# Two-layer decoder trunk on one core: three value products per key block in one bank, three score banks, no row sums on GpSimd

## The chip, the cores and the metric

The kernel runs on one core of a Trainium2 chip. The metric is device time in microseconds (us) of one execution, the median over several. Engines are called by the names of the profile: PE is TensorE (PEld its weight loads), DVE is VectorE, ACT is ScalarE, POOL is GpSimd, SP is SyncE, which issues most of the DMAs.

## What is computed

Two layers over 2048 tokens of width 1024. Layer 0 is a gated linear recurrence beside a pooling mixer. Layer 1 is causal attention with 16 heads of 64, where a key's weight also carries a forget term. The change touches layer 1 (and one helper that all weights pass). Cut to that:

```python
logf = jax.nn.log_sigmoid(fl + b_f)
cumf = jnp.cumsum(logf, axis=1).transpose(0, 2, 1)
...
logits = (jnp.einsum('bhqd,bhkd->bhqk', q[:, :, q0:q1], k[:, :, :q1]) * scale
          + cumf[:, :, q0:q1, None] - cumf[:, :, None, :q1])
mask = jnp.arange(q0, q1)[:, None] >= jnp.arange(q1)[None, :]
probs = jax.nn.softmax(jnp.where(mask, logits, -jnp.inf), axis=-1)
outs.append(jnp.einsum('bhqk,bhkd->bhqd', probs, v[:, :, :q1]))
...
o = o * jax.nn.silu(g)
return o @ w_out
```

## The kernel before, in words

The 2048 tokens go through in four segments of 512 (SEG). Each segment passes layer 0 and then layer 1, so the timeline alternates: a layer-0 stage of some 300 us, then an attention stage that grows with the segment, since segment s attends to s + 1 segments of keys.

Matrix products run in a format that keeps part of the mantissa (fp32r). To keep more of it, an operand is held as a first part (a rounded copy) and a second part (what the rounding left); a product of two such operands takes three matmuls. The helper `split_lo` (L184) makes a second part: full value minus first part. Its engine is DVE unless another is named.

**Weights.** `prep_w` brings one weight tile (1024 x 256) in four DMAs of 128 x 512 (`raw`). For each, ACT casts the first part (L295) and `split_lo` makes the second one. Pieces 1 and 3 of a tile go to POOL, pieces 0 and 2 to DVE (tile 0 wholly to POOL). Two tiles `wt` exist; `next_w` starts the load of the tile after the one that it hands out.

**Attention** (`attend`, L1116) runs per head over key blocks of 128 keys by 512 queries, 4(s + 1) blocks; the last four of a head lie on the diagonal and have 512, 384, 256 and 128 queries. Per block: two matmuls write the scores into a bank of PSUM (`pst`, two such banks; on the diagonal a third matmul adds the mask); ACT takes the exponential twice, once rounded (`ph`, L1153) and once in place (L1154); DVE subtracts to get the second part `pl`; two blocks later (LAG) the values are multiplied. The values are held with 130 columns: 64 second parts, 64 first parts and two columns of ones. Two products do it:

```python
mm(po[:, q0:], vv[:, b, 0:P], ph[:, q0:], start=(kb == 0), stop=end)
mm(pol[0:HD + 2, q0:], vv[:, b, HD:], pl[:, q0:],
   start=(kb == 0), stop=end)
```

The bank `po` (tile `pov`) then holds both halves of value x `ph` on separate partitions, and the bank `pol` first value x `pl` and, in a row of its own, the sum of `pl`. The sum of `ph` over the keys is kept apart: POOL adds each block's `ph` into `la` (L1160 to L1164), and the reduction over the 128 partitions is left to `finish`. At the end of a head DVE adds the row of `pol` to `la` (L1176) and puts the three value parts together (L1177, L1178), ACT rounds `la` (`lh`, L1180), and DVE makes its second part (`ll`). `finish` (L1184), run for a pair of heads, sums `lh` and `ll` of both heads over the partitions with four matmuls against `pairr` (`pL`), takes the reciprocal on ACT and multiplies.

**What goes on beside it.** `max_pass` does the scores of the next head with queries and keys changed about (`pmx`), from which DVE takes the row maximum (L1102, L1104). `prep` (L1054) makes the queries and keys of the head after that (ACT and DVE). `quad_attention` yields once per key block, and `weave` puts pieces of other projections between (`pqk`, `pgt`, `pv`, then `py`), in steps of 24 matmuls or 12. Within each engine the order is fixed when the program is built: a scheduler places instructions by priority and by its own estimate of when an operand is there.

**PSUM** has eight banks: two `pj` for projections, two `mx` (row maximum and small things), two `st`, one `o` and one `o2`. Layer 0 uses `st`, `mx` and `o` for the recurrence; `out_first` holds four banks for the first output tiles, one of them `o2`.

Of the kernel before, what the change touches and what calls it, by code (L numbers as in the profile page):

```python
# [35 lines left out]
def trunk(ctx, tc, x, cvec, norm_g, ada_c, ada_w, ada_b, ada_bg, lbp, w0, w0o, w1, w1f, w1o,  # L36
# [4 lines left out]
    def mm(*a, **k):  # L41
        return nc.tensor.matmul(*a, **k)  # L42
# [25 lines left out]
    def tmp(name, dt=F32, shape=(P, 512)):  # L68
        return tp.tile(list(shape), dt, name=name, tag="tmp")
# [5 lines left out]
        return ps.tile([P, 512], F32, name=name, tag="pj", bufs=2)  # L75

    def ps_st(name):
        return ps.tile([P, 512], F32, name=name, tag="st", bufs=2)

    def ps_o(name):  # L80
        return ps.tile([P, 512], F32, name=name, tag="o", bufs=1)

    def ps_o2(name):
        return ps.tile([P, 512], F32, name=name, tag="o2", bufs=1)

    def ps_mx(name):
        return ps.tile([P, 512], F32, name=name, tag="mx", bufs=2)
# [1 line left out]
    def f(ap):  # L89
        return ap.bitcast(F32)  # L90
# [21 lines left out]
    eps1 = cp.tile([P, 1], F32, name="eps1")  # L112
    V.memset(eps1, EPS)

    pairr = cp.tile([P, 3 * HD], F32R, name="pairr")
    of = tmp("of")[:, 0:3 * HD]
    V.memset(of, 0.0)
    V.memset(of[:, HD:2 * HD], 1.0)
    V.tensor_copy(pairr, of)

    NL = 7
    lmask = cp.tile([P, NL, P // 2], U8, name="lmask")
# [60 lines left out]
    def split_lo(out_t, full, hi, eng=None):  # L183
        (eng or V).tensor_tensor(out_t, full, f(hi), op=ALU.subtract)  # L184
# [93 lines left out]
    def prep_w(n):  # L278
        if n >= len(wseq) or n in wready:
            return  # L280
        late = wseq[n][0] == "e"
        src = None if late else wsrc[wseq[n][0]][wseq[n][1]]
        wt = wp.tile([P, 2, ND, 256], F32R, name="wt", tag="wt")
        parts = range(3 if late else 4)
        if not late and n >= len(wseq) - 5:
            parts = range((NEARLY[wseq[n][1]] + 1) // 2)
        for h in parts:
            sl = slice(2 * h, 2 * h + 2)
            raw = wp.tile([P, 2, 256], F32, name="raw", tag="raw", bufs=4)
            nc.sync.dma_start(raw, w1o[h][:, ND - 2:, :] if late else src[:, sl, :])  # L290
            if late:
                V.tensor_tensor(raw, raw, grow1[0][:, h * 256:(h + 1) * 256].unsqueeze(1).to_broadcast([P, 2, 256]),
                                op=ALU.mult)
            tc.cur_priority += 80
            S.copy(wt[:, 0, sl, :], raw)  # L295
            split_lo(wt[:, 1, sl, :], raw, wt[:, 0, sl, :], G if (h % 2 or n == 0) and n < len(wseq) - 2 else V)
            tc.cur_priority -= 80
        wready[n] = wt

# [520 lines left out]
    def out_first(s):  # L820

        L = seg0[s]
        xs = L["x"] = []
        for tb in range(NTB):
            xt = xp.tile([P, D], F32, name="xo", tag="xs")
            nc.sync.dma_start(xt, x[s * SEG + tb * P:s * SEG + (tb + 1) * P, :])
            xs.append((xt, once([P, 4], f"ss{tb}")))
        wt = next_w(("b", 0))

        L["py"] = wt, [(ps_pj, ps_pj, ps_o2, ps_mx)[tb]("py")[:, 0:256] for tb in range(NTB)]  # L830
        for tb in range(NTB):
            assert L["cores"] >= 3
            proj_N(L["py"][1][tb], wt, L["mix"], tb, (4, 5, 6, 7, 0, 1, 2), last=False)
            yield
# [281 lines left out]
    def attend(s, h):  # L1116
# [3 lines left out]
        Q1, Q3, K1, K2 = L["ops", h]  # L1120
        pair, j = h // 2, h % 2
        vc = L["v", pair]
        la = kp.tile([P, SEG], F32, name="la", tag="la", bufs=1)
        po, pol = ps_o("pov"), ps_o2("pol")
        nkb = NTB * (s + 1)
        kb = 0
        todo = []

        def values(b, q0, kb, vv, ph, pl):
            end = kb == nkb - 1  # L1130
            mm(po[:, q0:], vv[:, b, 0:P], ph[:, q0:], start=(kb == 0), stop=end)
            mm(pol[0:HD + 2, q0:], vv[:, b, HD:], pl[:, q0:],
               start=(kb == 0), stop=end)

        for c in range(s + 1):
            if c < s:
# [7 lines left out]
            for b in range(NTB):  # L1144
# [9 lines left out]
                S.activation(st[:, q0:], st[:, q0:], AF.Exp)  # L1154
                pl = tmp("pl", F32R)
                split_lo(pl[:, q0:], st[:, q0:], ph[:, q0:])
                if kb == 0:
                    first = f(ph)
                    if s == 0:
                        G.tensor_copy(la, first)  # L1160
                elif kb == 1 and s > 0:
                    G.tensor_tensor(la, first, f(ph), op=ALU.add)
                else:
                    G.tensor_tensor(la[:, q0:], la[:, q0:], f(ph[:, q0:]), op=ALU.add)  # L1164
                todo.append((b, q0, kb, vv, ph, pl))
                if len(todo) > LAG:
                    values(*todo.pop(0))
# [3 lines left out]
            values(*t)  # L1171
        if j == 0:
            L["u", pair] = xp.tile([P, 2, SEG], F32, name="u", tag="xs")
        u = L["u", pair][j * HD:(j + 1) * HD, 0, :]
        S.copy(u, po[HD:P])
        V.tensor_tensor(la[0:1], pol[HD:HD + 1], la[0:1], op=ALU.add)  # L1176
        V.tensor_tensor(u, po[0:HD], u, op=ALU.add)  # L1177
        V.tensor_tensor(u, pol[0:HD], u, op=ALU.add)  # L1178
        lh, ll = tmp("lh", F32R), tmp("ll", F32R)
        S.copy(lh, la)  # L1180
        split_lo(ll, la, lh)
        L["l", h] = (lh, ll)

    def finish(s, h):  # L1184

# [3 lines left out]
            return  # L1189
        u, rl = L["u", pair][:, 0, :], L["u", pair][:, 1, :]  # L1190
        pL = ps_misc("pL")
        for i in range(2):
            for part in range(2):
                mm(pL, pairr[:, (1 - i) * HD:(1 - i) * HD + P], L["l", h - 1 + i][part], start=(i + part == 0), stop=(i + part == 2))
        S.activation(rl, pL, AF.Ln)
        S.activation(rl, rl, AF.Exp, scale=-1.0)
        mix = L["mix"]
# [190 lines left out]
```

## Time and profile before

| | |
|---|---|
| median of 3 runs (lowest to highest) | 3030.41 us (3029.74 to 3030.75) |
| the profiled execution: its own time, its span | 3029.48 us, 3027.8 us |
| mean granted TensorE clock | 0.975 |
| busy: PE, PEld | 93%, 79% of the span |
| busy: DVE, ACT, POOL | 76%, 60%, 39% of the span |
| attention stages (us from the start) | 390 to 697, 998 to 1394, 1692 to 2172, 2473 to 3007 |

PE's matmuls are pipelined: a matmul of 512 columns is listed with some 0.4 us, but the next starts earlier; what one costs is read from start to start in the timeline. So a busy PE has losses in it that the idle time doesn't show. A weight load (PEld) goes with each matmul and carries the wait where the stationary operand is late. The granted clock has two levels in these records, 1.00 (2.4 GHz) and 0.50 (1.2 GHz); a mean between them is a mix of the two.

### The profile page before, as it was taken

Reading aid. Unit: us, or ns where it says so; the run is one execution under the profiler, and the core shown is the slowest. Engines: PE = TensorE matmul, PEld = TensorE weight load, DVE = VectorE, ACT = ScalarE, POOL = GpSimd, SP = SyncE. Lnnn points to the kernel's source line nnn. Section 1 sums busy time; section 2 is a strip of 40 time slices with the busy share of each in tenths; the row PEclk is TensorE's granted clock in tenths of the full one; section 3 lists DMA queues with packets and bytes.
Section 4 is the critical chain, followed back from the end, with each engine's and each line's share of the span. In section 5 each row is a group of like instructions: output and inputs, shape, how many; then the busy total and the mean of one; then the engine's idle time right before and its main releaser. Section 6 shows DMA issues by size and latency. Waiting matters only on the chain.

```text
span 3027.8 us, 49244 instructions
## 1 busy us (share of the span) xinstructions
PE 2808.9 (93%) x17212; PEld 2390.2 (79%) x17212; DVE 2301.3 (76%) x4390; ACT 1826.4 (60%) x3743; POOL 1172.5 (39%) x992
## 2 busy tenths in 40 slices
PE   4699999989999999989999999998999999999998
PEld 3688887879888887868878887776898877777777
DVE  8667678776676788886586788889667678888886
ACT  3344566774445666775455676768635467777774
POOL 3111233323211444444212355554432136566665
PEclk9899999999999999999999999999999999999999
DMA  7523365534233444533333443553342334333442
GB/s 246 174 57 102 106 141 139 119 91 124 79 102 110 119 119 104 131 99 115 100 95 116 122 124 115 126 133 113 97 126 71 114 104 115 105 113 107 113 138 86
DMA packets 207888, 348.97 MB, mean 115 GB/s; under 512 B 24068, under 2 KB 70788, under 8 KB 205080
## 3 DMA queue, kind: packets, MB, share of 16 engines
q1 hardware_dynamic: 201816, 329.03, 39.0%
q10 hardware_dynamic: 5824, 16.79, 1.7%
q8 instruction: 137, 2.24, 0.3%
q14 instruction: 111, 0.91, 0.1%
HBM read 293.58 MB, written 52.14 MB: 114 GB/s over the span
## 4 chain that ended last, share of the span: by engine, by line
PE 60%; DVE 19%; ACT 11%; DMA 4%; issue 4%; POOL 1%; SPq 0%; ACTq 0%; DVEq 0%; POOLq 0%
PE py L42 10%; PE pgt L42 8%; PE pqk L42 8%; PE pst L42 6%; PE pv L42 6%; PE pmx L42 4%; PE pov L42 3%; PE pol L42 3%; PE pf L42 3%; PE pq L42 3%; PE pl L42 3%; DVE pl L184 2%; DVE wt L184 2%; ACT wt L295 1%; DMA raw<-in_w_dram 1%
## 5 line engine op out<-in xcount | busy, mean ns | idle before, releaser
L184 POOL TENSOR_TENSOR wt<-raw,wt 128x512 fp32r<-128x512 f32 x287 | 419.5, 1470 | 1030.9 <-ACT wt L295 975.1
L1164 POOL TENSOR_TENSOR la<-la,ph 128x512 f32<-128x512 f32 (+3 forms) x528 | 610.6, 1156 | 385.7 <-ACT ph L1153 342.9
L184 DVE TENSOR_TENSOR pl<-pst,ph 128x512 fp32r<-128x512 f32 (+3 forms) x640 | 386.9, 605 | 133.4 <-ACT pst L1154 102.2
L1153 ACT ACTIVATE ph<-pst 128x512 fp32r<-128x512 f32 (+3 forms) x640 | 340.6, 532 | 235.1 <-PE pst L42 224.9
L42 PE MATMUL pqk<-wt,h 128*128 128x256 f32 x3072 | 433.1, 286 | 5.5 <-DVE h L497 2.7
L42 PEld LDWEIGHTS pqk<-wt,h 128*128 128x128 f32 x3072 | 411.9, 192 | 25.2 <-DVE h L497 3.5
L42 PE MATMUL pgt<-h,wt 128*128 128x512 f32 x1536 | 403.9, 405 | 0.0
L295 ACT CAST wt<-raw 128x512 fp32r<-128x512 f32 x578 | 335.2, 621 | 74.9 <-PE py L42 33.3
L42 PE MATMUL pv<-wt,h 128*128 128x256 f32 x2304 | 345.0, 298 | 10.7 <-DVE h L184 6.6
L42 PEld LDWEIGHTS pv<-wt,h 128*128 128x128 f32 x2304 | 326.1, 204 | 28.9 <-DVE h L184 9.6
L42 PEld LDWEIGHTS pgt<-h,wt 128*128 128x128 f32 x1536 | 293.1, 194 | 63.2 <-issue 1.9
L1154 ACT ACTIVATE pst<-pst 128x512 f32<-128x512 f32 (+3 forms) x640 | 340.0, 531 | 0.0
L184 DVE TENSOR_TENSOR wt<-raw,wt 128x512 fp32r<-128x512 f32 x291 | 265.7, 918 | 73.4 <-ACT wt L295 71.9
L1102 DVE TENSOR_REDUCE mxs<-pmx 128x1 f32<-128x512 f32 x384 | 258.6, 684 | 20.3 <-PE pmx L42 17.2
L42 PE MATMUL py<-wt,o 128*128 128x256 f32 x1536 | 202.2, 286 | 1.4 <-ACT o L1200 1.2
L42 PE MATMUL py<-wt,mix 128*128 128x256 f32 x1536 | 198.2, 287 | 2.3 <-DVE yt L844 2.1
L42 PEld LDWEIGHTS py<-wt,o 128*128 128x128 f32 x1536 | 192.8, 192 | 6.7 <-ACT o L1200 1.5
L42 PEld LDWEIGHTS py<-wt,mix 128*128 128x128 f32 x1536 | 187.9, 191 | 9.8 <-issue 4.5
L42 PE MATMUL pst<-Q,K1o 128*128 128x512 f32 x384 | 162.6, 424 | 23.2 <-DVE pl L184 21.7
L42 PE MATMUL pmx<-K2o,Q 67*128 67x512 f32 x384 | 162.0, 426 | 21.9 <-ACT Q L1077 10.2
L42 PE MATMUL pov<-ph,Vo 128*128 128x512 f32 x384 | 162.8, 425 | 6.6 <-ACT ph L1153 6.2
L1104 DVE CUSTOM_DVE_ANT_0 pmx<-pmx,mq 128x128 f32<-128x128 f32 (+3 forms) x256 | 124.6, 497 | 55.6 <-PE pmx L42 53.8
(251 smaller groups left out, 5309.1 us busy)
## 6 DMA issues: line engine op xcount, KB each, us to landing
raw<-in_w_dram SPq DMA_DIRECT2D x448, 256.0 KB, 3.5
K2o<-k2d SPq DMA_DIRECT2D x192, 160.0 KB, 3.4
Vo<-vd SPq DMA_DIRECT2D x96, 260.0 KB, 2.7
K1o<-k1d SPq DMA_DIRECT2D x96, 256.0 KB, 3.4
raw<-in_w1o_dram SPq DMA_DIRECT2D x66, 256.0 KB, 3.6
raw<-in_w0o_dram SPq DMA_DIRECT2D x64, 256.0 KB, 3.2
vd<-Vc SPq DMA_DIRECT2D x48, 260.0 KB, 8.1
ada<-in_ada_w_dram ACTq DMA_DIRECT2D x12, 1024.0 KB, 5.0
```

Source lines behind the costliest of these rows:

```text
L42: return nc.tensor.matmul(*a, **k)
L184: (eng or V).tensor_tensor(out_t, full, f(hi), op=ALU.subtract)
L295: S.copy(wt[:, 0, sl, :], raw)
L1102: V.tensor_reduce(mxs[:, i, c:c + 1], pm[:, 0:n], axis=AX.X, op=ALU.max)
L1104: V.tensor_tensor_reduce(pm[:, 0:n], pm[:, 0:n], mq[:, SEG - n:], 1.0, NEG, op0=ALU.add, op1=ALU.max, accum_out=mxs[:, i, c:c + 1])
L1153: S.activation(ph[:, q0:], st[:, q0:], AF.Exp)
L1154: S.activation(st[:, q0:], st[:, q0:], AF.Exp)
L1164: G.tensor_tensor(la[:, q0:], la[:, q0:], f(ph[:, q0:]), op=ALU.add)
```

## The change

Each key block has three value products, all into one bank: first parts of the values with the ones by `ph`, second parts by `ph`, first parts with the ones by `pl`. The bank then holds the finished values and the finished denominator in row 64, so POOL's adds, `la`, `pol` and the sums behind them go. At the end of a head ACT copies the denominator's first part and the values, and DVE makes the denominator's second part; both are rows of one tile `sums` (rows 0 and 32 for the even head, 64 and 96 for the odd one, zeros between), and `finish` needs one matmul. The bank that `pol` had becomes a third score bank; `out_first` takes a score bank in its place. From the fifth weight tile on, all second parts are made on POOL (the last two tiles of the list excepted).

```diff
     def ps_st(name):
-        return ps.tile([P, 512], F32, name=name, tag="st", bufs=2)
+        return ps.tile([P, 512], F32, name=name, tag="st", bufs=3)
...
-    def ps_o2(name):
-        return ps.tile([P, 512], F32, name=name, tag="o2", bufs=1)
...
-    pairr = cp.tile([P, 3 * HD], F32R, name="pairr")
-    of = tmp("of")[:, 0:3 * HD]
+    pairr = cp.tile([P, P], F32R, name="pairr")
+    of = tmp("of")
     V.memset(of, 0.0)
-    V.memset(of[:, HD:2 * HD], 1.0)
-    V.tensor_copy(pairr, of)
+
+    sums = cp.tile([P, SEG], F32R, name="sums")
+    V.tensor_copy(sums, of)
+    V.memset(of[0:HD, 0:HD], 1.0)
+    V.memset(of[HD:P, HD:P], 1.0)
+    V.tensor_copy(pairr, of[:, 0:P])
...
-            split_lo(wt[:, 1, sl, :], raw, wt[:, 0, sl, :], G if (h % 2 or n == 0) and n < len(wseq) - 2 else V)
+            split_lo(wt[:, 1, sl, :], raw, wt[:, 0, sl, :], G if (h % 2 or n == 0 or n >= NPRO) and n < len(wseq) - 2 else V)
...
-        L["py"] = wt, [(ps_pj, ps_pj, ps_o2, ps_mx)[tb]("py")[:, 0:256] for tb in range(NTB)]
+        L["py"] = wt, [(ps_pj, ps_pj, ps_st, ps_mx)[tb]("py")[:, 0:256] for tb in range(NTB)]
...
-        la = kp.tile([P, SEG], F32, name="la", tag="la", bufs=1)
-        po, pol = ps_o("pov"), ps_o2("pol")
+        po = ps_o("pov")
...
-            mm(po[:, q0:], vv[:, b, 0:P], ph[:, q0:], start=(kb == 0), stop=end)
-            mm(pol[0:HD + 2, q0:], vv[:, b, HD:], pl[:, q0:],
-               start=(kb == 0), stop=end)
+            mm(po[0:HD + 2, q0:], vv[:, b, HD:], ph[:, q0:], start=(kb == 0), stop=False)
+            mm(po[0:HD, q0:], vv[:, b, 0:HD], ph[:, q0:], start=False, stop=False)
+            mm(po[0:HD + 2, q0:], vv[:, b, HD:], pl[:, q0:], start=False, stop=end)
...
-                if kb == 0:
-                    first = f(ph)
-                    if s == 0:
-                        G.tensor_copy(la, first)
-                elif kb == 1 and s > 0:
-                    G.tensor_tensor(la, first, f(ph), op=ALU.add)
-                else:
-                    G.tensor_tensor(la[:, q0:], la[:, q0:], f(ph[:, q0:]), op=ALU.add)
...
-        u = L["u", pair][j * HD:(j + 1) * HD, 0, :]
-        S.copy(u, po[HD:P])
-        V.tensor_tensor(la[0:1], pol[HD:HD + 1], la[0:1], op=ALU.add)
-        V.tensor_tensor(u, po[0:HD], u, op=ALU.add)
-        V.tensor_tensor(u, pol[0:HD], u, op=ALU.add)
-        lh, ll = tmp("lh", F32R), tmp("ll", F32R)
-        S.copy(lh, la)
-        split_lo(ll, la, lh)
-        L["l", h] = (lh, ll)
+        r = j * HD
+        hi = sums[r:r + 1]
+        S.copy(hi, po[HD:HD + 1])
+        S.copy(L["u", pair][r:r + HD, 0, :], po[0:HD])
+        split_lo(sums[r + 32:r + 33], po[HD:HD + 1], hi)
...
-        for i in range(2):
-            for part in range(2):
-                mm(pL, pairr[:, (1 - i) * HD:(1 - i) * HD + P], L["l", h - 1 + i][part], start=(i + part == 0), stop=(i + part == 2))
+        mm(pL, pairr[0:97], sums[0:97], start=True, stop=True)
```

The scheduler gives PE another order. In the last attention stage, within one head, PE's rows were these (`pst` scores, `pov` and `pol` values, `pmx` the next head's row maximum, `pqk` a projection put between; an x stands before the number of equal rows):

```order
L42 MATMUL pst<-Q_28174,K1o 128x512
L42 MATMUL pst<-Q_28175,K2o 128x512
L42 MATMUL pol<-pl,Vo 66x512
L42 MATMUL pmx<-K2o,Q_28569 128x512
L42 MATMUL pov<-ph,Vo 128x512
L42 MATMUL pqk<-wt,h_25908 128x256
L42 MATMUL pst<-Q_28174,K1o 128x512
```

At the same place, PE's rows are now:

```order
L42 MATMUL pst<-Q_27775,K2o 128x512
L42 MATMUL pqk<-wt,h_25535 128x256 x24
L42 MATMUL pst<-Q_27774,K1o 128x512
L42 MATMUL pst<-Q_27775,K2o 128x512
L42 MATMUL pov<-ph,Vo 66x512
L42 MATMUL pov<-ph,Vo 64x512
L42 MATMUL pov<-pl,Vo 66x512
L42 MATMUL pmx<-K2o,Q_28160 128x512
L42 MATMUL pst<-Q_27774,K1o 128x512
```

A block has six matmuls of its own instead of five, and the projection's matmuls, which stood one to five at a time between the blocks, now stand in whole steps of 24 with several blocks between two steps.

POOL's rows at the beginning of the first attention stage were these:

```order
L184 TENSOR_TENSOR wt<-raw,wt 128x512 x12
L1160 COPY la<-ph 128x512
L184 TENSOR_TENSOR wt<-raw,wt 128x512 x2
L1164 TENSOR_TENSOR la<-la,ph 128x384
L1164 TENSOR_TENSOR la<-la,ph 128x256
L1164 TENSOR_TENSOR la<-la,ph 128x128
```

They are now (`Vc` is the ones beside the values of a pair of heads):

```order
L185 TENSOR_TENSOR wt<-raw,wt 128x512 x32
L1034 CAST Vc<-one_107 128x8x2
L185 TENSOR_TENSOR wt<-raw,wt 128x512 x8
L1034 CAST Vc<-one_107 128x8x2
L185 TENSOR_TENSOR wt<-raw,wt 128x512 x6
```

The row sums are gone from POOL's queue, and every piece of a weight tile is in it.

## Rows read from the trace of the kernel before

**Rows 1.** The page: busy time of each engine (1), the chain by engine (4).

```profile
PE 2808.9 (93%) x17212; PEld 2390.2 (79%) x17212; DVE 2301.3 (76%) x4390; ACT 1826.4 (60%) x3743; POOL 1172.5 (39%) x992
...
PE 60%; DVE 19%; ACT 11%; DMA 4%; issue 4%; POOL 1%; SPq 0%; ACTq 0%; DVEq 0%; POOLq 0%
```

**Rows 2.** Windows by stage: PE, PEld, DVE, ACT, POOL busy; clock, DMA share, GB/s.

```profile
390.00:697.00 307.00, 284.51 (x1836) 245.74 (x1834) 235.77 (x472) 213.27 (x448) 99.74 (x101) 0.98 0.46 117
697.00:998.00 301.00, 291.96 (x1991) 264.89 (x1990) 204.13 (x400) 141.06 (x294) 72.35 (x53) 0.98 0.38 108
998.00:1394.00 396.00, 366.30 (x2135) 302.41 (x2135) 314.20 (x588) 279.60 (x578) 174.18 (x150) 0.97 0.43 111
1692.00:2172.00 480.00, 448.00 (x2460) 358.72 (x2459) 396.84 (x715) 348.65 (x707) 257.46 (x214) 0.97 0.45 121
2473.00:3007.00 534.00, 509.26 (x2800) 402.81 (x2798) 451.35 (x805) 391.94 (x777) 341.63 (x277) 1.00 0.39 111
```

**Rows 3.** Timeline of PE, last attention stage: start, duration, what.

```profile
2605.25 0.28 PE L42 MATMUL pov<-ph,Vc 128*128 128x256 f32 x1
2605.37 0.27 PE L45 MATMUL pmt<-ident,m 128*1 128x128 f32 x1
...
2620.86 0.39 PE L42 MATMUL pst<-Q,K2o 67*128 67x512 f32 x1
2621.09 0.39 PE L42 MATMUL pol<-pl,Vo 128*66 128x512 f32 x1
2621.32 0.39 PE L42 MATMUL pov<-ph,Vo 128*128 128x512 f32 x1
```

**Rows 4.** Waits of PE's weight loads: us in total, times, longest.

```profile
PEld pst L42 <- DVE pl L184: 59.4, 78, 2.6
PEld pov L42 <- ACT ph L1153: 26.3, 73, 2.5
...
PEld pmx L42 <- ACT Q L1077: 20.4, 36, 1.7
PEld pol L42 <- DVE pl L184: 17.6, 41, 1.2
PEld pst L42 <- ACT Q L1114: 15.1, 32, 2.3
```

**Rows 5.** Windows in and after one stall in the second attention stage; columns as in rows 2.

```profile
1150.90:1153.30 2.40, 0.02 (x1) 0.00 (x0) 2.40 (x4) 1.76 (x4) 2.23 (x3) 1.00 0.68 184
1155.00:1157.00 2.00, 2.00 (x11) 2.00 (x11) 2.00 (x4) 0.32 (x1) 1.43 (x1) 0.50 0.54 135
```

**Rows 6.** Timeline of all engines across that stall.

```profile
1149.66 2.97 POOL L184 TENSOR_TENSOR wt<-raw,wt 128x512 fp32r<-128x512 f32 x2
...
1150.26 1.25 DVE L1199 TENSOR_TENSOR u<-u,sg 128x512 f32<-128x512 f32 x1
...
1151.43 1.24 DVE L172 TENSOR_TENSOR t_qk<-t_qk,ms_qk 128x16 f32<-128x16 f32 x1
...
1152.59 0.68 DVE L184 TENSOR_TENSOR pl<-pst,ph 128x512 fp32r<-128x512 f32 x1
...
1153.32 0.74 PE L42 MATMUL pst<-Q,K 128*128 128x512 f32 x2 [2.40 <-DVE pl L184]
```

**Rows 7.** Timeline of DVE in the third attention stage, while POOL does nothing.

```profile
1823.05 0.16 DVE L174 TENSOR_TENSOR ssq<-t_qk,r_qk 128x16 f32<-128x16 f32 x1
```

**Rows 8.** The page's groups (5): busy, mean ns of one, idle before.

```profile
L184 POOL TENSOR_TENSOR wt<-raw,wt 128x512 fp32r<-128x512 f32 x287 | 419.5, 1470 | 1030.9 <-ACT wt L295 975.1
L1164 POOL TENSOR_TENSOR la<-la,ph 128x512 f32<-128x512 f32 (+3 forms) x528 | 610.6, 1156 | 385.7 <-ACT ph L1153 342.9
...
L1153 ACT ACTIVATE ph<-pst 128x512 fp32r<-128x512 f32 (+3 forms) x640 | 340.6, 532 | 235.1 <-PE pst L42 224.9
...
L184 DVE TENSOR_TENSOR wt<-raw,wt 128x512 fp32r<-128x512 f32 x291 | 265.7, 918 | 73.4 <-ACT wt L295 71.9
```

**Rows 9.** Groups of DVE in the layer-0 stage from 697 to 998 us.

```profile
L184 DVE TENSOR_TENSOR wt<-raw,wt 128x512 fp32r<-128x512 f32 x39 | 34.5, 886 | 11.9 <-ACT wt L295 11.9
```

## The prediction

> **What bounds the kernel now.** The page first: PE is busy 93% of the span, DVE 76%, and 60% of the chain that ended last is PE, 19% DVE [rows 1]. So PE's work sets the time, and DVE is the engine that holds PE up. Next the windows by stage [rows 2]: in the four attention stages together (1717 us) PE is idle for 109 us (307 - 284.5, 396 - 366.3, 480 - 448.0, 534 - 509.3), while DVE is busy for 77 to 85% of each. In a layer-0 stage PE is idle for 9 of 301 us. Idle time is too little a measure, since a listed matmul hides the tail of the one before. The loads' waits show more [rows 4]: they waited 59.4 + 17.6 = 77.0 us for DVE's `pl`, 26.3 us for ACT's `ph` and 20.4 + 15.1 = 35.5 us for ACT's `Q`. Last the clock: the three earlier attention stages have a mean granted clock of 0.98, 0.97 and 0.97, the last one 1.00 [rows 2]. One stall shows how these hang together. PE waited 2.40 us for `pl` [rows 6], and DVE was busy all the while; a moment later, with PE at work again, the granted clock was 0.50, the 1.2 GHz level [rows 5]. DVE was late because of two jobs with both inputs in SBUF: a 128x16 product took 1.24 us and a 128x512 one 1.25 us beside a 2.97 us stretch of POOL [rows 6], while a 128x16 product took 0.16 us when POOL did nothing [rows 7].
>
> **What it costs PE.** From start to start, a matmul of 512 columns takes 0.23 us, with 66 stationary columns as with 128 [rows 3]; one of 256 takes 0.12 us [rows 3]. So a third product costs a whole matmul, though it has half the output. There are 640 key blocks: 16 heads x (4 + 8 + 12 + 16). Off the diagonal 384 x 0.23 = 88.3 us. On it, 64 of each width: 0.23 + 0.18 (between the two measured widths) + 0.12 + 0.12 (the 128 columns taken like 256) = 0.65, x 64 = 41.6 us; with 0.12 to 0.23 for the second and 0.06 to 0.12 for the last it is 34 to 45 us. `finish` loses three of four matmuls per pair: 32 x 3 x 0.23 = 22.1 us. Net **+108 us** (100 to 111). Nothing hides it, since PE is the path.
>
> **What it gives back in the attention stages.** The ceiling is what PE waits there.
> - `pl`, 77.0 us. With two banks the scores of block i + 2 wait for `pl` of block i; between stand one block's matmuls and the fills. With three, `pl` of block i is first needed by the third product, after the scores of i + 2: by the order that is 14 matmuls, 3.2 us, against two exponentials and a subtraction, 0.53 + 0.53 + 0.68 = 1.7 us [rows 6, 8] and three handovers. Before, eight matmuls and some fills (1.9 to 2.4 us) had to cover the same. DVE gets lighter too: 610.6 of POOL's 1172.5 us are row sums [rows 1, 8], and DVE's long products are long beside POOL's; at a head's end four DVE jobs become one. I take 65 us; bounds 0 and 77.
> - the clock: at 1.2 GHz half the time is lost, so a mean clock c loses (1 - c) of the stretch: 307 x 0.02 + 396 x 0.03 + 480 x 0.03 = 32.4 us. The dips follow the stalls, and the last stage has none. I take 24; bounds 0 and 32.
> - `Q`, 35.5 us: ACT's rounding of `la` no longer waits for POOL's last sum ahead of the next head's work. Part of the wait is ACT's own work. I take 18; bounds 0 and 35.5.
> - `ph`, 26.3 us: a third bank lets scores be made earlier, and there is a matmul more to cover the exponential. I take 16; bounds 0 and 26.3.
>
> Together 123 us (ceiling 171).
>
> **The other stages.** A layer-0 stage loses 39 splits on DVE, 34.5 us of its 204 [rows 2, 9]; POOL, busy for 72 of 301 us, gets 39 x 1.47 = 57 us more [rows 2, 8]. A weight tile then takes POOL 4 x 1.47 = 5.9 us, not 2.9, against 96 x 0.12 = 11.5 us of PE per tile, with the next tile loaded ahead: hidden, except where two tiles are taken at once (the last two of layer 0's output). PE's slack here is 9 us of idle and 6 us of clock (301 x 0.02); I take 1.5 us off each of three stages and nothing off the first (bounds: 15 us off each, 23 us on each). The ones for `v` (POOL's `Vc`) can hold weights behind them while a buffer is in use; that cover is the same 11.5 us per tile. The copies of single rows at a head's end take the place of whole-tile copies on ACT: nothing.
>
> **Sum.** Own time of the profiled execution 3029.5 (span 3027.8 and 1.7 around it; 0.9 under the median shown) + 108 - 123 - 4.5 = 3010 us.
>
> **Two rules of the skill.** Rows 6 and 7 show DVE's product stretched to the length of POOL's instruction. The Trainium skill, SBUF — State Buffer, "Who interferes with whom", states it as a lock: a DVE instruction with two SBUF inputs contends with a GpSimd instruction that reads SBUF, and the second to issue fully blocks until the first finishes. The trace agrees (1.24 us against 0.16 us). For attention this speaks for the change. For layer 0 it speaks against it, since 39 more POOL instructions per stage each may block a DVE product; that is rival 2. The stall and the clock [rows 5] agree with the Trainium skill, TensorE: Matmul & The Clock Gate, "What's actually happening": an idle PE is throttled to 1.2 GHz. By that rule alone all 32 us come back if the stalls go; I keep 24, since PE may still stall for other reasons, and the sum by the rule would be 3002 us.
>
> **The rivals.**
> 1. *PE's new order brings the waits back.* PE's row of six matmuls per block is 6 x 0.23 = 1.4 us. DVE needs `pl`, 0.68 us, and a row maximum of about the same length per block, 1.36 us. The projection's matmuls, which stood between the blocks, now come 24 at a time. In between, DVE has 0.04 us per block for keys, norms and gates; what it doesn't get done waits for the burst, and PE waits with it. Against it: about 1 us more of cover for `pl`. If only half of the 123 us comes back, the time is 3029.5 + 108 - 62 = 3075 us, slower. It decides if PE's loads still wait over some 40 us for `pl`.
> 2. *The lock moves to layer 0.* If each of 39 splits per stage blocks a DVE product for its 1.47 us, DVE does 57 - 34.5 = 23 us more per stage where the recurrence's products feed PE. With half of that on the path in four stages: 3010 + 46 = 3056 us, slower. For it: rows 6. Against it: DVE is busy for 68% there and PE's waits are short.
> 3. *All of it comes back.* With DVE under 75% and POOL nearly empty in attention, waits for `pl`, `ph` and the clock go wholly and those for `Q` mostly (160 us), and layer 0 gains 5 us a stage: 3029.5 + 108 - 160 - 15 = 2962 us. For it: the last stage runs at full clock already.
> 4. *Weights come late* where two tiles are taken at once: POOL's 5.9 us instead of 2.9 us in four stages, 3 us each: 3010 + 12 = 3022 us. This is also where the change does little.
>
> **How the numbers follow.** Forecast 52%, rivals 17, 9, 16 and 6%. A measurement of this kernel can tell about 0.2%, 6 us, from no change. Of the forecast's share some three quarters lie under 3024, the rest is split evenly; rival 3 is faster, 1 and 2 slower, 4 half faster and half within. Faster 0.57, within 0.12, slower 0.31. The range leaves out the end of rival 3 and the far half of rival 1: 2960 to 3072 us.
>
> **What would show it.** Right: waits of PE's loads for `pl` under 20 us, granted clock of at least 0.99 in all attention stages, no stretch in which a 128x16 product of DVE takes over 1 us there, PE's idle time in attention under 60 us although 544 matmuls more run. Attention stages: the first two shorter by some 10 us each, the third shorter by a few, the last longer by 10 to 20, since it has 256 of the 640 blocks and no lost clock to give back. Wrong: `pl` still over 40 us (rival 1), layer-0 stages over 310 us (rival 2), PE waiting for `wt` from POOL (rival 4), or matmuls of 66 or 64 stationary columns into the shared bank that take over 0.25 us from start to start, which would make the first term too small.

## The result: slower by 3.1%, and the profile after

| | before | after |
|---|---|---|
| median (lowest to highest) | 3030.58 us (3029.74 to 3039.66, 4 runs) | 3127.12 us (3122.61 to 3130.07, 4 runs) |
| ratio, 95% interval | | 1.0310 (1.0285 to 1.0335) |
| profiled execution: own time, span | 3029.48, 3027.8 us | 3122.61, 3120.8 us |

The forecast was 3010 us with a range up to 3072; the time lies 117 us over the one and 55 us outside the other. The page of after, beside [rows 1] and [rows 8]: busy time of each engine, the chain by engine and by line, the costliest group.

```profile
PE 2877.7 (92%) x17756; PEld 2426.0 (78%) x17756; DVE 1966.2 (63%) x3922; ACT 1823.0 (58%) x3743; POOL 819.5 (26%) x678
...
PE 52%; ACT 9%; issue 7%; DVE 7%; DMA 6%; POOL 2%; ACTq 0%; SPq 0%; POOLq 0%; DVEq 0%
PE pov L42 9%; PE pgt L42 7%; PE pqk L42 6%; PE pst L42 6%; PE py L42 6%; DMA K2o<-k2d 4%; PE pv L42 4%; PE pmx L42 4%; PE pf L42 2%; PE pq L42 2%; POOL wt L185 2%; PE pl L42 2%; DMA xt<-in_x_dram 1%; ACT wt L296 1%; ACT Q L1074 1%
...
L185 POOL TENSOR_TENSOR wt<-raw,wt 128x512 fp32r<-128x512 f32 x565 | 750.6, 1349 | 2061.6 <-ACT wt L296 1907.2
```

DVE lost 335 us and POOL 353 us of work, and the kernel is slower all the same. PE got 69 us more of listed work, and its share of the chain fell from 60 to 52%, so it isn't PE's added work alone. New among the costliest of the chain is a load, `K2o` (4%): the second of the two tiles in which a chunk of 512 stored keys is read back. It holds the keys' first parts and the rows of the forget term, and `pst` and the next head's `pmx` work with it.

Windows by stage (columns as in [rows 2]); the lines are attention and layer 0 in turn, the first layer-0 part (0 to 396) left out:

```profile
396.00:713.00 317.00, 290.52 (x1882) 251.23 (x1881) 176.48 (x394) 213.00 (x449) 86.80 (x71) 0.97 0.45 114
713.00:1025.00 312.00, 292.03 (x1991) 264.67 (x1991) 192.90 (x358) 141.37 (x293) 118.95 (x91) 0.98 0.36 105
1025.00:1415.00 390.00, 373.50 (x2245) 303.35 (x2244) 237.30 (x509) 279.10 (x579) 87.71 (x73) 0.99 0.42 113
1415.00:1725.00 310.00, 290.07 (x1973) 263.22 (x1972) 193.74 (x358) 139.47 (x290) 115.17 (x88) 0.97 0.36 104
1725.00:2215.00 490.00, 465.32 (x2628) 364.97 (x2627) 313.94 (x636) 346.96 (x706) 87.93 (x73) 0.99 0.43 118
2215.00:2526.00 311.00, 292.49 (x1983) 265.10 (x1982) 195.65 (x363) 140.38 (x291) 115.15 (x88) 0.97 0.33 99
2526.00:3098.00 572.00, 541.70 (x3009) 419.90 (x3008) 381.11 (x730) 390.40 (x777) 81.92 (x68) 0.99 0.36 104
```

Two things are to be seen. Every layer-0 stage is some 10 us longer though DVE has less to do there (193 us; 204 in [rows 2]). And the last attention stage took 572 us instead of 533, with 30 us in which PE is idle (25 before).

The waits of PE and its loads, beside [rows 4]:

```profile
PEld pst L42 <- DMA K2o<-k2d: 48.3, 37, 3.3
PE pst L42 <- DMA K2o<-k2d: 34.9, 33, 3.1
PE pl L42 <- DVE Dt L595: 32.8, 11, 4.8
PEld pov L42 <- DVE pl L185: 27.3, 62, 3.8
PEld pst L42 <- ACT Q L1115: 20.5, 35, 2.5
PEld pov L42 <- ACT ph L1153: 20.0, 24, 4.4
PEld pmx L42 <- ACT Q L1078: 14.6, 39, 1.0
```

The 77.0 us for DVE's `pl` are 27.3 now. Those for `Q` stand where they were (35.1; 35.5 before). On top stand two waits that were smaller before: `K2o`, and in layer 0 the product `Dt` (here `pl` is a bank of layer 0's recurrence, not attention's tile). The same two in the kernel before:

```profile
PEld pst L42 <- DMA K2o<-k2d: 3.3, 7, 1.3
PE pl L42 <- DVE Dt L594: 14.0, 8, 2.7
```

In the last attention stage of after, the time that PE and its loads stood idle until a load of `K2o` had landed (the two overlap):

```profile
  DMA K2o<-k2d: 59.7, 49
```

The same stage of the kernel before:

```profile
  DMA K2o<-k2d: 4.6, 8
```

### The profile page after: what moved, and what is told of

The parts are those of the page before. It is cut to its first block, busy times and chain, and to the rows that moved or that the text cites. A ratio compares the mean times of both kernels' runs of the same rounds, so it can differ in the third digit from the quotient of the medians.

```text
span 3120.8 us, 48664 instructions
## 1 busy us (share of the span) xinstructions
PE 2877.7 (92%) x17756; PEld 2426.0 (78%) x17756; DVE 1966.2 (63%) x3922; ACT 1823.0 (58%) x3743; POOL 819.5 (26%) x678
## 4 chain that ended last, share of the span: by engine, by line
PE 52%; ACT 9%; issue 7%; DVE 7%; DMA 6%; POOL 2%; ACTq 0%; SPq 0%; POOLq 0%; DVEq 0%
PE pov L42 9%; PE pgt L42 7%; PE pqk L42 6%; PE pst L42 6%; PE py L42 6%; DMA K2o<-k2d 4%; PE pv L42 4%; PE pmx L42 4%; PE pf L42 2%; PE pq L42 2%; POOL wt L185 2%; PE pl L42 2%; DMA xt<-in_x_dram 1%; ACT wt L296 1%; ACT Q L1074 1%
## 5 line engine op out<-in xcount | busy, mean ns | idle before, releaser
L185 POOL TENSOR_TENSOR wt<-raw,wt 128x512 fp32r<-128x512 f32 x565 | 750.6, 1349 | 2061.6 <-ACT wt L296 1907.2
L42 PE MATMUL pqk<-wt,h 128*128 128x256 f32 x3072 | 423.4, 288 | 3.7 <-DVE h L498 2.3
L42 PE MATMUL pgt<-h,wt 128*128 128x512 f32 x1536 | 392.7, 399 | 0.0
L42 PE MATMUL pv<-wt,h 128*128 128x256 f32 x2304 | 330.0, 293 | 4.7 <-DVE h L185 2.5
L42 PEld LDWEIGHTS pv<-wt,h 128*128 128x128 f32 x2304 | 312.4, 199 | 19.4 <-DVE h L185 4.5
L42 PE MATMUL pov<-ph,Vo 128*66 128x512 f32 (+1 forms) x768 | 250.9, 403 | 10.0 <-ACT ph L1153 10.0
L42 PE MATMUL py<-wt,mix 128*128 128x256 f32 x1536 | 205.7, 291 | 5.0 <-DVE yt L845 2.8
L42 PE MATMUL pst<-Q,K2o 67*128 67x512 f32 x384 | 157.9, 417 | 39.3 <-DMA K2o<-k2d 34.9
L591 ACT ACTIVATE Dt<-Dt 128x512 f32<-128x512 f32 x112 | 70.3, 631 | 171.2 <-DVE Dt L590 169.3
L42 PE MATMUL pst<-Q,K1o 128*128 128x512 f32 x384 | 154.9, 408 | 0.0
```

Of the source, the lines that this page charges most:

```text
L591: S.activation(Dt, Dt, AF.Exp)
```

## The experiments

Stage lengths in us, read from each trace between the first and the last score matmul of each attention stage (A1 to A4) and the layer-0 stages between them (L2 to L4; L1 is all ahead of A1):

| | L1 | A1 | L2 | A2 | L3 | A3 | L4 | A4 |
|---|---|---|---|---|---|---|---|---|
| before | 389.7 | 307.6 | 300.8 | 396.5 | 297.2 | 480.0 | 301.8 | 533.2 |
| after | 396.3 | 316.9 | 311.7 | 389.8 | 310.4 | 490.1 | 310.5 | 572.1 |
| third product alone | 390.9 | 316.5 | 300.6 | 419.8 | 297.1 | 510.1 | 301.0 | 583.1 |
| all weights on POOL alone | 398.7 | 311.7 | 310.7 | 406.2 | 310.3 | 483.6 | 314.4 | 555.1 |
| extra POOL jobs in layer 0 | 401.1 | 310.7 | 309.4 | 398.0 | 307.0 | 480.4 | 308.6 | 535.5 |
| no row sums | 389.7 | 308.0 | 300.8 | 378.1 | 297.3 | 456.4 | 300.5 | 510.0 |
| after, weights halved | 388.7 | 315.1 | 300.4 | 382.2 | 297.5 | 484.5 | 299.4 | 558.8 |
| after, four `K2o` | 392.3 | 311.0 | 320.9 | 387.3 | 314.2 | 478.8 | 310.9 | 535.6 |
| after, both of these | 389.4 | 312.1 | 300.0 | 385.3 | 297.9 | 481.4 | 299.1 | 535.1 |

### One part of the change alone

**All weights on POOL**, in the kernel before:

```diff
-G if (h % 2 or n == 0) and n < len(wseq) - 2 else V
+G if (h % 2 or n == 0 or n >= NPRO) and n < len(wseq) - 2 else V
```

> The kernel before, with only one part of the change: all second parts of the weights on POOL. Theory A: the layer-0 stages grow by 8 to 13 us each, to 308 us or more, and the whole to 3055 to 3080 us, since in attention POOL now has row sums and all weights. Rival (the order, not the lock): 3020 to 3040 us.

Measured: 3122.66 us, ratio 1.0325 (1.0299 to 1.0351). This line by itself costs as much as the whole change. Each of L2 to L4 is 10 to 13 us longer, as expected. The total is not: the attention stages, where POOL has the row sums besides, grow too, A2 by 10 us and A4 by 22.

**The third product alone**: the kernel before with each block's first product split in two; row sums, banks and `finish` as they were.

```diff
-            mm(po[:, q0:], vv[:, b, 0:P], ph[:, q0:], start=(kb == 0), stop=end)
+            for w in ((HD, 0) if kb == 0 else (0, HD)):
+                n = HD + 2 if w else HD
+                mm(po[0:n, q0:], vv[:, b, w:w + n], ph[:, q0:], start=(kb == 0 and w > 0), stop=(end and w > 0))
...
-        S.copy(u, po[HD:P])
+        S.copy(u, po[0:HD])
...
-        V.tensor_tensor(u, po[0:HD], u, op=ALU.add)
```

> The kernel before, with a third value product per block and one DVE addition less at a head's end; row sums on POOL, two score banks and divided weights stay. If PE's work is the path and nothing gives it back: 130 us more, 3150 to 3165 us. If the third product fills time in which PE waits for DVE anyway: 30 to 90 us more, 3060 to 3120 us, with waits of PE's loads for pl under 40 us (77 before).

Measured: 3138.26 us, ratio 1.0372 (1.0350 to 1.0394), about 113 us, between the two ranges. Its waits:

```profile
PEld pst L42 <- DVE pl L184: 68.5, 95, 3.0
PEld pol L42 <- DVE pl L184: 23.2, 47, 1.4
```

PE's added work is paid in the main (113 of the 130 us counted), and the waits for `pl` are longer than in [rows 4], not shorter: more matmuls on PE cover nothing by themselves.

**No row sums**: the kernel before, with `la` set to ones once per head, so the sum of `ph` over the keys is not in the denominator.

```diff
                 if kb == 0:
-                    first = f(ph)
...
-                    G.tensor_tensor(la[:, q0:], la[:, q0:], f(ph[:, q0:]), op=ALU.add)
+                    G.memset(la, 1.0)
```

> The kernel before without POOL's row sums: POOL sets la to ones once per head, so the sum of ph over the keys is left out of the denominator; two score banks and two value products as before, weights halved between DVE and POOL. If the row sums were what held DVE up in attention (the lock, and POOL's last sum ahead of the next head's queries), POOL falls by some 600 us, the waits for pl fall under 40 us (77 before), those for Q under 20 us (35.5 before), and the time is 2950 to 2990 us. If the two banks were what held PE up, the waits for pl stay at 60 us or more and the time is 3010 to 3030 us. Layer-0 stages stay within 3 us of before in both.

Measured: 2960.71 us, ratio 0.9772 (0.9753 to 0.9790). The waits for `pl`:

```profile
PEld pst L42 <- DVE pl L184: 18.2, 48, 1.8
...
PEld pol L42 <- DVE pl L184: 15.8, 36, 1.2
```

77.0 us fall to 34.0 with two score banks as before. So it was mainly POOL's row sums, and not the number of banks, that made DVE late. The waits for `Q`, expected under 20 us, are 31.6: the row sums were not what held these up. They cost 69 us; the way the change gets rid of them costs 113.

### Layer 0

**The change with its weights halved again** (the line of the first experiment undone):

> The changed kernel, with the weights' second parts divided between POOL and DVE as before; all else as changed. Theory A (all splits on POOL stretch DVE's products in layer 0): the three later layer-0 stages, now 311 us each, return to 298 to 303 us, and DVE's Dt products to their means of before (656, 512 ns); the whole comes to 3085 to 3100 us. Rival (the layer-0 stages are longer because of the order that the scheduler gives PE, or because the first output tile now holds a score bank): they stay at 308 us or more, and the whole within 15 us of 3127.

Measured: 3049.49 us, ratio 1.0078 (1.0058 to 1.0098), some 70 us less than the change. L2 to L4 are back at 297 to 300 us. That is more than was expected, since the attention stages fall too: by the table 43 us come from L1 to L4 and 28 from A1 to A4. What POOL did to them is seen at the start of the recurrence, here in after (timeline: start, duration, what, and in brackets the idle time ahead and what ended it):

```profile
782.33 5.69 POOL L185 TENSOR_TENSOR wt<-raw,wt 128x512 fp32r<-128x512 f32 x4
...
782.57 1.51 DVE L590 TENSOR_TENSOR Dt<-cT 128x256 f32<-128x256 f32 x1
...
784.00 1.49 DVE L589 TENSOR_TENSOR Dt<-cT 128x256 f32<-128x256 f32 x1
...
785.41 1.48 DVE L590 TENSOR_TENSOR Dt<-cT 128x256 f32<-128x256 f32 x1
786.81 1.48 DVE L589 TENSOR_TENSOR Dt<-cT 128x256 f32<-128x256 f32 x1
...
788.22 0.41 DVE L593 TENSOR_TENSOR Dt<-qT,Dt 128x256 f32<-128x256 f32 x1
...
789.11 1.77 PE L42 MATMUL pl<-Dt 128*127 128x64 f32 x8 [4.81 <-DVE Dt L595]
```

The same place in the kernel before:

```profile
766.84 2.89 POOL L184 TENSOR_TENSOR wt<-raw,wt 128x512 fp32r<-128x512 f32 x2
767.09 1.51 DVE L589 TENSOR_TENSOR Dt<-cT 128x256 f32<-128x256 f32 x1
...
768.52 1.49 DVE L588 TENSOR_TENSOR Dt<-cT 128x256 f32<-128x256 f32 x1
...
769.93 0.41 DVE L589 TENSOR_TENSOR Dt<-cT 128x256 f32<-128x256 f32 x1
...
771.50 0.81 PE L42 MATMUL pl<-Dt 128*127 128x64 f32 x5 [2.67 <-DVE Dt L594]
```

Four POOL jobs in a row of 1.42 us each (5.69 / 4) turn four DVE products of 0.41 us into 1.5 us; two turn two. PE waits 4.81 us for the end of that row of products instead of 2.67. In the whole of L2, PE's waits for `Dt` go from 4.2 to 9.0 us, and its idle time from 9.0 to 20.0; the rest of that lies in small waits for other tiles of DVE and ACT, which no run takes apart. But a weight that comes late from POOL would also fit the longer stages, so two runs separate them.

**Zeros written by POOL**: the change, but for the pieces of layer-0 weights that DVE had before, POOL writes zeros twice instead of subtracting, so these second parts are left out. It then reads nothing from SBUF there.

```diff
+            if h % 2 == 0 and NPRO <= n < len(wseq) - 2 and wseq[n][0] in "ab":
+                for _ in range(2):
+                    G.memset(f(wt[:, 1, sl, :]), 0.0)
+            else:
+                split_lo(wt[:, 1, sl, :], raw, wt[:, 0, sl, :], G if (h % 2 or n == 0 or n >= NPRO) and n < len(wseq) - 2 else V)
```

> The changed kernel, but for the weights of layer 0 and of its output from the fifth tile on, the pieces that DVE had made before are not made: POOL writes zeros there, twice, so that it is busy but reads nothing (half of these second parts are left out). DVE is relieved as in the change. If POOL's reading is what stretches DVE's products (theory A): layer-0 stages 296 to 303 us, Dt means at or under those of before (656, 512, 441, 418 ns), the whole 3080 to 3095 us. If the longer queue on POOL or PE's new order is the cause: layer-0 stages stay at 307 us or more.

Measured: 3071.46 us, ratio 1.0143 (1.0115 to 1.0171); L2 to L4 300.9, 298.6 and 299.6 us, and PE's wait at that place 2.67 us again. The mean times of the four `Dt` products were expected at or under those of before; over the whole run these are 619, 518, 438 and 428 ns, and all four were over them (693, 548, 500, 458 ns). POOL still made 55 second parts in L2 (40 before, 79 after), since the attention weights stayed with it; so it is not the mean length of the products that goes with the stage's length. A zero written is also ready earlier than a second part, so this run alone doesn't exclude lateness; nor does it exclude that DVE's lighter load helped (177 us busy in L2, 204 before).

**Extra POOL jobs in layer 0**: the kernel before, where DVE goes on making its pieces and POOL gets as many jobs again whose output nobody reads.

```diff
+            if h % 2 == 0 and NPRO <= n < len(wseq) - 2 and wseq[n][0] in "ab":
+                la = kp.tile([P, SEG], F32, name="la", tag="la", bufs=1)
+                hi = f(wt[:, 0, sl, :])
+                G.tensor_tensor(la.rearrange("p (a c) -> p a c", a=2), hi, hi, op=ALU.subtract)
```

> The kernel before, with one more POOL job for every piece of a layer-0 weight tile that DVE makes: first part minus itself, 128x512 from two inputs in SBUF, into a tile that nobody reads. DVE still makes the second part, so no weight comes from POOL that did not before. If the lock is what made layer 0 longer with all weights on POOL, the three later layer-0 stages grow again, by 8 us or more each (300 to 308 and over), DVE's short products take over 1 us in them, and the time is 3060 us or more. If it was the weights that came late from POOL, the stages stay within 3 us of before, and the time is 3025 to 3045 us.

Measured: 3073.81 us, ratio 1.0140 (1.0120 to 1.0160). L2 to L4 grew by 8.6, 9.8 and 6.8 us, L1 by 11.4; the attention stages stand within 4 us. L4 misses the 8 us expected by one. The place again:

```profile
781.30 1.22 POOL L300 TENSOR_TENSOR la<-wt 128x512 f32<-128x512 f32 x1
...
781.54 1.26 DVE L593 TENSOR_TENSOR Dt<-cT 128x256 f32<-128x256 f32 x1
782.48 1.46 POOL L184 TENSOR_TENSOR wt<-raw,wt 128x512 fp32r<-128x512 f32 x1
782.72 1.50 DVE L592 TENSOR_TENSOR Dt<-cT 128x256 f32<-128x256 f32 x1
...
787.62 1.94 PE L42 MATMUL pl<-Dt 128*127 128x64 f32 x8 [4.34 <-DVE Dt L598]
```

No weight comes from POOL here that did not before. Those that do stand behind the added jobs and can be later, but PE and its loads waited only 2.0 + 2.9 us for them in the whole run, and its loads 7.0 us for ACT's first parts (2.4 before), where L1 to L4 grew by 36.6 us. So lateness can be about a quarter of it at most; what is left is that POOL's jobs hold up DVE's products. The DVE product even has the length of the POOL job beside it, 1.26 us beside 1.22 and 1.5 beside 1.42 to 1.46.

### The stored keys

**The change with four `K2o` buffers** instead of three (and 8 temporaries instead of 9, for the memory):

```diff
-tag="k2o", bufs=3)
+tag="k2o", bufs=4)
-name="tp", bufs=9
+name="tp", bufs=8
```

> The changed kernel with four buffers instead of three for the key rows K2o that are read back, and eight instead of nine temporary tiles (to make room). Theory B (blocks now follow each other without projection matmuls between, so that a chunk's four blocks pass faster than the next K2o can be loaded into the one free buffer): PE's waits for K2o fall from 35 us to under 8 us, the last attention stage from 572 to under 550 us, the whole to 3080 to 3095 us. Rival (K2o is late because SP's queue is held up by other transfers): waits for K2o stay over 20 us and the whole over 3115 us.

Measured: 3074.43 us, ratio 1.0158 (1.0132 to 1.0184), some 46 us less than the change. No wait for `K2o` is left among those of PE and its loads, and A3 and A4 fall by 11 and 37 us (L2 and L3 are 9 and 4 us longer). The last stage:

```profile
2515.00:3051.00 536.00, 530.20 (x3011) 416.25 (x3010) 380.17 (x730) 390.07 (x775) 81.92 (x68) 1.00 0.37 111
```

PE is idle for 6 of 536 us, at full clock. A stall as it was in after (PE and SP's queue):

```profile
2897.46 0.32 SPq L1138 DMA_DIRECT2D K1o<-k1d  x1
...
2897.93 2.15 SPq L1089 DMA_DIRECT2D K2o<-k2d  x2
...
2902.20 0.50 PE L42 MATMUL pst<-Q,K2o 67*128 67x512 f32 x1 [1.22 <-DMA K2o<-k2d]
```

The matmul's semaphore is that of the first of the two `K2o` loads, issued at 2897.93: from there to the matmul pass 4.27 us. Before `K1o`, SP had waited 10 us for PE to be done with a buffer. The weights' loads stand in the same queue of SP: for a `raw` buffer that POOL still reads it waited

```profile
SPq L291 <- POOL wt L185: 1174.5, 477, 19.6
```

in after; in the kernel before it was

```profile
SPq L290 <- DVE wt L184: 470.3, 116, 17.8
SPq L290 <- POOL wt L184: 423.0, 229, 18.2
```

together 893 us. With the weights halved the wait of the loads for `K2o` is 35.2 us instead of 48.3. SP then waits 495.6 + 464.8 = 960 us for `raw`, near the 893 of before, where the loads waited 3.3 us for `K2o`. So the slower release of `raw` is not enough to explain it. Two things have a part. Of the 48.3 us, 32.2 (20 waits of 37) are for loads that SP issued in an unbroken row behind a weights' load that had waited for POOL; with the weights halved it is 19.2 of 35.2 (13 of 36). And with the projection's matmuls in whole steps, PE passes faster through the first chunk of a head: in the last stage it takes 7.7 us in the mean with four buffers, from the chunk's first score matmul to the next chunk's, and 11.0 before (the second chunk 8.2 and 7.8). That the buffers were too few is shown; how the 46 us divide between the two is not.

**The same four buffers in the kernel before**, as a control:

> The kernel before, with four K2o buffers and eight temporary tiles, as a control: its loads wait for K2o for only 3 us, so the fourth buffer should do nothing there: 3022 to 3036 us. If it gains 15 us or more, the gain of the other runs with four buffers belongs to the buffers and not to the changed kernel.

Measured: 3035.11 us, ratio 1.0013 (0.9996 to 1.0029): the buffer is worth nothing where nobody waits for it.

### Both cures, and what is left

**Weights halved and four `K2o` buffers**:

> The changed kernel with both causes taken away: weights' second parts divided between POOL and DVE as before, four K2o buffers and eight temporary tiles. If the two causes add up: layer-0 stages 298 to 302 us, K2o waits of PE's loads under 8 us, last attention stage under 530 us, the whole 3000 to 3020 us, which is faster than before by 0.3 to 0.9%. If the K2o waits were only the visible end of another limit: 3030 to 3050 us.

Measured over 12 runs: 3021.64 us (3016.51 to 3028.56), ratio 0.9975 (0.9963 to 0.9988), 8 us under the kernel before, and just over the range expected; A4 is 535 us, not under 530. Windows of its first and last attention stage:

```profile
389.00:701.00 312.00, 287.83 (x1880) 248.62 (x1878) 197.24 (x427) 213.55 (x448) 46.41 (x38) 0.98 0.45 116
...
2465.00:3000.00 535.00, 530.09 (x3007) 415.28 (x3006) 398.03 (x759) 389.19 (x775) 48.20 (x38) 1.00 0.38 111
```

**The same, with the attention weights alone on POOL** (`and wseq[n][0] in "cd"` behind `n >= NPRO`):

> The run before this with both causes taken away, but with all second parts of the attention layer's weights (input and output) on POOL, halves only for layer 0's. If SP, held up by POOL's slower release of the raw pieces, is what made attention dearer with all weights on POOL: about the same as with halves everywhere plus 5 to 25 us. If a DVE that is freed in attention helps now that K2o is early: 5 to 20 us less than with halves everywhere.

Measured: 3041.22 us, ratio 1.0040 (1.0026 to 1.0054), some 20 us more. A1 to A4 are 317, 388, 481 and 535 us, 7 us more together; L2 to L4 are 305, 301 and 306 us, 15 us more, since the first of these tiles are loaded while layer 0 still runs (of the 39 pieces that DVE has in such a stage [rows 9] the run with extra jobs found 26 to be layer 0's own). POOL isn't free for weights even there.

**The same, with two score banks** (the third one given back to `out_first` alone):

> The kernel with halved weights and four K2o buffers (3021.6 us), with two score banks instead of three. Theory (the prediction's): the waits for pl went because the third bank lets two blocks of scores stand ahead; with two banks the loads wait again over 40 us for pl, the attention stages grow by 40 to 80 us together, and the time is 3065 to 3100 us. Rival: the waits went because DVE and POOL have less to do beside each other (no row sums); then two banks are enough, the waits for pl stay under 20 us, and the time is 3015 to 3035 us.

Measured: 3031.67 us, ratio 1.0013 (1.0002 to 1.0024). The loads' waits for `pl` are then

```profile
PEld pst L42 <- DVE pl L188: 21.2, 67, 1.2
PEld pov L42 <- DVE pl L188: 20.6, 48, 1.1
```

41.8 us instead of 26.5. The waits came back as the theory had them, and the price was the rival's: by the ratios 0.4%, some 11 us, not 40 to 80. The third bank gives a small part.

**Ones in a spare column**: two products and two banks as before, and the sum of `ph` taken from PE without a third product. The second part of one value column of the 64 of each head is left out, and ones stand in its place. Denominators and `finish` are as in the change.

```diff
+            G.tensor_copy(vc[:, :, :, 0:2], one1.unsqueeze(1).unsqueeze(1).to_broadcast([P, NTB, 2, 2]))
...
-                split_lo(vcs[pj][:, 2 * t2:2 * t2 + 2, :, 0:HD], src, hi)
+                split_lo(vcs[pj][:, 2 * t2:2 * t2 + 2, :, 1:HD], src[:, :, :, 1:], hi[:, :, :, 1:])
...
+        S.copy(la, po[0:1])
+        V.tensor_tensor(pol[HD:HD + 1], pol[HD:HD + 1], la, op=ALU.add)
+        V.memset(po[0:1], 0.0)
```

> The kernel before, two products and two score banks, with the sum of ph taken from PE without a third product: the second part of one value column of the 64 of each head is left out (its value stays rounded) and a column of ones stands in its place, so that row 0 of the bank of values is the sum of ph. POOL's row sums go as in the run without them; the denominator's two parts stand in rows as in the change, and finish needs one matmul instead of four. If the run without row sums told the price of the row sums (2960.7 us) and PE is the path, the time is 2960.7 less up to 22 us of finish: 2935 to 2960 us. If the head's end, now a chain of single-row jobs (sum, its two parts, the copies), holds the values' bank longer, the time is 2965 to 2990 us and PE waits at each head's first value product.

Measured: 2999.74 us (2991.38 to 3008.06), ratio 0.9892 (0.9859 to 0.9924): 1.1% under the kernel before, and the fastest version that has a whole denominator, at the price that one column in 64 has values of one part. It hits neither range. It is 39 us over the run without row sums, though it has 96 matmuls less, and two waits of its loads are longer or new:

```profile
PEld pov L42 <- ACT ph L1157: 37.5, 105, 3.8
...
PEld pst L42 <- DMA K2o<-k2d: 18.5, 14, 4.7
```

Whether the head's end or the loads of `K2o` hold it up stays open; it wasn't tried with four buffers.

## Why the prediction was wrong

117 us were missed: 44 in layer 0 (-4.5 forecast, +39.4 measured: 6.6 + 10.9 + 13.2 + 8.7), 69 in attention with the tail (108 - 123 = -15 forecast, +53.5 measured), and 4 because the profiled execution lies under the median.

**The step that failed in layer 0** is the one that took 1.5 us off each of three stages. It looked for a tile that is ready too late (4 x 1.47 us against 11.5 us of PE) and found it hidden, which is right: PE and its loads waited 2.7 + 1.1 us for `wt` from POOL in all. But the cost of a POOL job was not its lateness; it is what it does to the DVE products beside it. The upper bound (23 us each) held the truth, the value was taken from the wrong end. Rival 2 named the mechanism and gave 11.5 us per stage (half of 23); measured were 6.6 to 13.2. It got 9%, because DVE was "busy for 68% there and PE's waits are short". Both are means over the stage. The place itself was in the trace of before: two POOL jobs, two products at 1.5 us, and PE waiting 2.67 us for them (shown above). Doubling that queue was to be read there. The Trainium skill, SBUF — State Buffer, "Who interferes with whom", says that the shared lock concerns a DVE instruction with two SBUF inputs against a GpSimd instruction that reads SBUF, not one that only writes it. The runs agree: 1.26 us beside a 1.22 us job that reads, and stages back at 299 to 301 us where POOL wrote zeros.

**The term for PE had the pitch right.** It is 0.23 us with 66 and with 64 stationary columns in the shared bank too, as these rows of the last attention stage of after show (2906.07 to 2906.29 to 2906.52, then two products to 2906.99):

```profile
2906.07 0.39 PE L42 MATMUL pst<-Q,K1o 128*128 128x512 f32 x1
...
2906.29 0.39 PE L42 MATMUL pst<-Q,K2o 67*128 67x512 f32 x1
...
2906.52 0.63 PE L42 MATMUL pov<-ph,Vo 128*66 128x512 f32 x2
...
2906.99 0.40 PE L42 MATMUL pov<-pl,Vo 128*66 128x512 f32 x1
```

The third product alone cost about 113 us where its count (88.3 + 41.6) gave 130, so the sum was 17 us too high. The 22 us taken off for `finish` were not measured by themselves.

**What attention gives back was right within a tenth in total, in part by luck, and something else took half of it.** With four `K2o` buffers A1 to A4 and the tail take 1735 us, 3 us less than before (1738): of 108 us about 111 came back, and 123 were forecast. With three buffers it is 1792 us. The step that failed in attention is the 57 us between, a wait that the prediction put at nothing: it did not ask what the loads of `K2o` need when PE passes faster through a chunk of keys and SP waits longer for the weights ahead of them. It had noted that the projection's matmuls no longer stood between the blocks; it counted this against DVE (rival 1), not for the loads. The wait was all but absent before, 4.6 us in the last stage, and A4, which has most of the old keys, is where most of it came.

**Term by term.** `pl`: 65 forecast; the loads' waits went from 77.0 to 27.3, so about 50. The reason was half wrong: the runs give the row sums' absence the main part (77.0 to 34.0 with two banks) and the third bank some 11 us of the time. The clock: the means are 0.97, 0.99, 0.99 and 0.99 against 0.98, 0.97, 0.97 and 1.00, so it came back in A2 and A3 and was lost in A1 and A4; with four `K2o` A4 is at 1.00. By the prediction's way of counting 8 of the 24 us came in after, and 17 with both cures (0.98, 0.99, 0.99 and 1.00). `Q`: 18 forecast, nothing came (35.5 to 35.1). `ph`: 16 forecast, 6 came (26.3 to 20.0). Together the terms come to some 73 us with both cures, of 110 that came back there; PE's idle time in attention fell by 50 us (109 to 59) and the clock gave 17, and the rest lies inside PE's busy time, where no view here takes it apart. So the agreement with 123 is no proof of the terms.

**The marks set for it.** PE's idle time in attention was to be under 60 us; it is 98 us in after, and 59 us with both cures. Layer-0 stages over 310 us were to speak for rival 2: they are 310 to 312. `pl` over 40 us was to speak for rival 1: it is 27.3, so its mechanism fell; its size came all the same (some 54 of 123 us came back in after), by another wait. The forecast's own marks were missed too: `pl` under 20 us, a clock of 0.99 in every attention stage (0.97 in A1), and no 128x16 product of DVE over 1 us there (8 of 84 were; 23 of 84 before). The stages were to be 10 us shorter twice, then a few shorter, then 10 to 20 longer; they are 9 longer, 7 shorter, 10 and 39 longer. Rival 3 (all comes back) falls with `Q`.

**The balance of the parts** (ratios times 3030 us): third product +113, row sums gone -69, third bank -11, `finish` -22 by count, together +11; the version with both cures is at -8, and the 19 us between belong to no part measured alone. All weights on POOL adds some 70 (98 in the kernel with row sums), `K2o` some 46; together they are 102 and not 116, since each is smaller when the other is gone (55 and 31). So the change does its own job, and nearly all of its gain pays for the third product; a line beside it, and a buffer count left as it was, made it slower.

## What to carry to other kernels

Price a job that is moved to GpSimd by the DVE products that run beside it, at the narrowest place of the stage and not by shares of busy time: find in the trace one place where the two already meet and ask what two more of them would do there. When a change takes out what stood between PE's blocks, ask which load now has less time, and count its buffers. And try each part of a combined change alone: here one part was worth 69 us and another cost 98.

## What was not expected of the hardware

What a POOL job costs DVE is paid per encounter and is repeatable: PE's wait at the first place was 4.81 or 4.82 us in all three later layer-0 stages of after and 4.81 us with all weights on POOL alone, 2.67 us before, with the weights halved and with zeros written. In the rows shown, a DVE product of 128x256 took 0.41 us when POOL was idle and the length of the POOL job when not, so the smaller the product, the larger the factor: 3.6 times here, and nearly 8 times for the 128x16 products of [rows 6] and [rows 7]. POOL's own jobs took 1349 ns in the mean after, 1470 before.
